# A decay mask moved from TensorE to GpSimd, and the last product's sums taken bank by bank

## The chip, the cores and the metric

The kernel runs on one core of a Trainium2 chip. Its engines are TensorE (PE, matmuls and transposes), VectorE (DVE), ScalarE (ACT), GpSimd (POOL) and SyncE (SP, which issues most of the transfers); each runs its own list of instructions in order, and they meet by semaphores. The metric is the device time of one execution, in microseconds (us).

## The reference

One decoder layer on a sequence of 1024 tokens of width 1024, in fp32. A norm and an input projection feed two groups of heads: differential attention (4 heads) and a gated DeltaNet (4 heads of width 128, in chunks of 64 tokens). Their outputs go through one output projection onto the residual, and a squared-ReLU MLP of hidden width 4096 follows. The parts that the change touches:

```python
g = jnp.cumsum(g, axis=-1)                      # log decay, summed within a chunk
gdiff = g[..., :, None] - g[..., None, :]
decay = jnp.where(tri, jnp.exp(jnp.where(tri, gdiff, 0.0)), 0.0)
Lmat = jnp.where(strict, jnp.einsum('bhncd,bhnjd->bhncj', k_beta, k) * decay, 0.0)
sol = lax.linalg.triangular_solve(Lmat, rhs, left_side=True, lower=True, unit_diagonal=True)
qk = jnp.where(tri, jnp.einsum('bhncd,bhnjd->bhncj', q, k) * decay, 0.0)
```

The MLP is the norm of x, a product with `w_up`, relu squared, a product with `w_down`, and the sum with x. The `decay` matrix is 1 on the diagonal, falls below it, and is 0 above it.

## The kernel before, in words

Every large product is made of three matmuls: each fp32 operand is split into a high and a low part (`hH`, `hL` for activations, `wH`, `wL` for weights), and high x high, low x high and high x low are summed in the same PSUM bank. The kernel works in chunks of 128 rows (P = 128), four to a tile of 512 columns. The stages, by the clock of the trace: 0 to 70 us the norm and the gates; 70 to about 235 the projections of the DeltaNet heads and what prepares their scan; then scan, attention and output projection interleaved until about 620; MLP up until 930; MLP down until the end.

**The decay factors.** A loop over the four heads and two halves (L746 to L760) makes eight tiles `dtm` of 128x512, one 128x128 block for each chunk. ScalarE scales the triangle `tri` by the log decays of the chunk, four instructions for the high parts (`rrh`) and four for the low ones (`rrl`, L752). Two matmuls with the constant triangle `gt_r` (L754, L755) turn them into sums of log decays between two rows, in a bank `ps_e`. Four more matmuls (L757), one for each 128 columns, add `caus`, which is -1e30 above the diagonal, by multiplying it with an identity, both in bf16. ScalarE takes the exponential (L759), so masked places become 0.

**Who reads them.** `dn_proj` (L671) makes the projections of kind 1 (k), 0 (q) and 2 (v) in this order. For each head and half it issues 24 matmuls into a bank `ps_dn` (L267 to L269), of which there are two; ScalarE copies the bank to `cp` (L683), ScalarE and VectorE make the convolution `cy` over four taps (L685, L687), and an activation follows. For k, VectorE makes `k2` (L780), TensorE transposes it (L735) and makes the gram product `ps_m` (L742), and VectorE multiplies the gram by `bp` and by `dtm` (L799), which gives `lt`. GpSimd makes `vsc` beside it (L806). `lt` is stored in blocks to DRAM (`fsx_d`); once all eight are there, `invert` loads them as `fx` (L766), runs 31 steps of two VectorE instructions (L770, L772) and stores the result. `horner` loads it as `gb` (L823), and its first matmuls are L829. For q, VectorE multiplies the gram by `bp` and `dtm` in the same way (L866), which gives `qk`. So `dtm` has two readers, both on VectorE.

**What sets the order.** The instructions of each engine in this stretch are put in order by the scheduler of the Tile framework (`TileContext(schedule_with_timeline_sim=True)`, L1963), which models the times of the program. Only the stretches in a `manual_schedule` (the first 70 us, part of the MLP) keep the order in which they are written; that of the MLP down holds TensorE's order alone. A change of one instruction can therefore move others.

**The end.** `down` (L1847) is one product of the MLP down; 14 of them, each of two halves `s`, use two sets of four banks in turn. `bankB` consists of two tiles of two banks, X1 and X0: t = 0, 1 lie in X1 and t = 2, 3 in X0. A half has 16 pairs (j, t), each of three matmuls (L1863 to L1865), t the bank and j a step of the contraction. In the last half of the last product (`final and s`) t is the outer loop, in all others j is. After the product, four VectorE additions (L1870) take the banks into `acc`, and in the last products a store follows each (L1872). Waits are kept for tiles, so an addition that reads one bank waits for what was issued before it on both banks of its tile, and a matmul into one bank waits for an addition that was issued before it and reads the other bank.

Of the kernel before, what the change touches and what calls it, by code (L numbers as in the profile page):

```python
# [10 lines left out]
F32R = mybir.dt.float32r  # L11
BF16 = mybir.dt.bfloat16
AF = mybir.ActivationFunctionType
ALU = mybir.AluOpType
# [4 lines left out]
P = 128  # L19
# [103 lines left out]
def tile_hymba_layer(  # L123
# [6 lines left out]
    nc = tc.nc  # L130
    V, S, G, T = nc.vector, nc.scalar, nc.gpsimd, nc.tensor

    x2 = x[0]
    out2 = out[0]
# [185 lines left out]
    gp = gpctx.enter_context(tc.tile_pool(name="gp", bufs=1))  # L320
# [147 lines left out]
    tri = sp.tile([P, P], F32, name="tri")  # L468
    gt_f = gp.tile([P, P], F32, name="gt_f")
# [90 lines left out]
    behind = ExitStack()  # L560
    for ins in mark + [x_last]:
        behind.enter_context(tc.issue_after(ins.ins))
    identb = const.tile([P, P], BF16, name="identb")
    V.tensor_copy(identb, ident)
    gt_r = gp.tile([P, P], F32R, name="gt_r")
    V.tensor_copy(gt_r, gt_f)
    caus = const.tile([P, P], BF16, name="caus")
    V.tensor_copy(caus, caus_f)

# [31 lines left out]
    v4 = lambda t: t.rearrange("p (c d) -> p c d", d=P)  # L601
# [59 lines left out]
    def ta(name, bufs, dt=F32):  # L661
        return sa.tile([P, 512], dt, tag=name, name=name, bufs=bufs)
# [66 lines left out]
    def bc_mask(t):  # L729
        return t.unsqueeze(1).broadcast_to([P, 4, P])  # L730
# [15 lines left out]
    for h in range(HEADS):  # L746
        for hf in range(2):
            rh, rl = ta("rrh", 1, F32R), ta("rrl", 1, F32R)
            for t, col in ((rh, ggh), (rl, ggl)):
                for c in range(4):  # L750
                    i = cidx(h, 4 * hf + c)
                    S.activation(t[:, c * P:(c + 1) * P], tri, AF.Copy, scale=col[:, i:i + 1])  # L752
            pse = ph.tile([P, 512], F32, tag="ph", name="ps_e")
            T.matmul(pse, gt_r, rh, start=True, stop=False)  # L754
            T.matmul(pse, gt_r, rl, start=False, stop=False)  # L755
            for c in range(4):
                T.matmul(pse[:, c * P:(c + 1) * P], caus, identb, start=False, stop=c == 3)  # L757
            dtm = sa.tile([P, 512], F32, name=f"dtm{h}{hf}")
            S.activation(dtm, pse, AF.Exp)  # L759
            dts[h, hf] = dtm  # L760

    def invert():
# [15 lines left out]
    for h, hf, y, th in skew(dn_proj(1)):  # L778
# [6 lines left out]
        for c in range(4):  # L785
            i = cidx(h, 4 * hf + c)
# [9 lines left out]
        for c in range(4):  # L796
            i = cidx(h, 4 * hf + c)
# [53 lines left out]
    for h, hf, q2 in skew(dn_proj(0)):  # L851
# [6 lines left out]
        for c in range(4):  # L858
            i = cidx(h, 4 * hf + c)
# [3 lines left out]
        for c in range(4):  # L863
            i = cidx(h, 4 * hf + c)
# [175 lines left out]
    late, accs, over = [], {}, set()  # L1040
# [769 lines left out]
    NK = FF // 2048  # L1810
# [21 lines left out]
    def u_raw(m):  # L1832
        if m < len(halves):
            kg, i, s = halves[m]
            g0 = 4 * kg + 2 * s
            return nc.sync.dma_start(urs[max(m - 1, 0) % 4].rearrange("p (g q) t -> p g q t", g=2),
                                     ud[i][g0:g0 + 2].rearrange("g p q t -> p g q t"))
# [5 lines left out]
    def split4(dst, src):  # L1843
        for j in (0, 2):
            split([x[:, j:j + 2] for x in dst], src[:, j:j + 2])

    def down(kg, wd, i, flip, n, out, start, stop):  # L1847
        bank = bankB if flip ^ (kg % 2) else bankA
        final = kg == NK - 1 and i == 4
        for s in range(2):  # L1850
            v = views[4 * (turn_of[0] % 2):][:4]
            turn_of[0] += 1
            m = halves.index((kg, i, s))
            raw = urs[max(m - 1, 0) % 4]
            split4(v[0:2], raw)
            split4(v[2:4], wd[n][s])
            u_raw(m + 4 if m else 1)
            seq = [(j, t) for t in range(4) for j in range(4)] if final and s else \
                [(j, t) for j in range(4) for t in range(4)]
            for j, t in seq:  # L1860
                sl = slice(t * P, t * P + P)
                s0, s1 = start and s == 0 and j == 0, stop and s == 1 and j == 3
                T.matmul(bank[t], v[0][:, j, sl], v[2][:, j], start=s0, stop=False, skip_group_check=True)  # L1863
                T.matmul(bank[t], v[0][:, j, sl], v[3][:, j], start=False, stop=False, skip_group_check=True)  # L1864
                T.matmul(bank[t], v[1][:, j, sl], v[2][:, j], start=False, stop=s1, skip_group_check=True)  # L1865
        half, ns = out
        for t in range(4):
            tb = t + (4 if half == 0 else 0)
            o = accs[tb][:, ns]
            V.tensor_tensor(o, o, bank[t], ALU.add)  # L1870
            if kg == NK - 1 and i in (2, 3, 7, 4):
                nc.sync.dma_start(out2[tb * P:(tb + 1) * P, ns], o)  # L1872

    u_raw(0)
    for n in "ab":
# [18 lines left out]
    for kg in range(NK):  # L1894
        wd = wds[kg]

        def both(dst, l, r):
            for s in range(2):
                V.tensor_tensor(wd[dst][s], wd[l][s], wd[r][s], ALU.subtract)

        down(kg, wd, 1, 0, "a", (0, lo), True, False)
        both("b", "b", "a")
        down(kg, wd, 5, 1, "b", (1, hi), True, False)
        both("b", "d", "b")
        down(kg, wd, 6, 0, "b", (0, hi), False, False)
        down(kg, wd, 3, 1, "d", (0, hi), False, True)
        both("a", "b", "a")
        down(kg, wd, 7, 0, "a", (1, hi), False, False)
        down(kg, wd, 2, 1, "c", (0, lo), True, True)
        if kg + 1 < NK:  # L1910
            for s in range(2):
                dn_raw(kg + 1, "a", s)
        both("b", "c", "b")
        down(kg, wd, 4, 0, "b", (1, lo), False, True)
        if kg + 1 < NK:
            for n in "bdc":
                for s in range(2):
                    dn_raw(kg + 1, n, s)
# [49 lines left out]
```

## Time and profile before

| | us |
|---|---|
| median of three runs (lowest, highest) | 1227.69 (1225.83, 1229.32) |
| the profiled execution | 1227.74 |
| span of its profile | 1226.0 |
| TensorE busy | 1208.2 |
| VectorE busy | 836.9 |
| ScalarE busy | 624.0 |
| GpSimd busy | 151.9 |

The span is what the profile covers; 1.74 us of the execution lie around it. Columns of the profile rows: start and duration, engine, line of the code, operation, output and inputs with their shapes; in brackets the idle time of that engine just before and what ended it. Matmuls are pipelined, so that the durations of neighbours overlap: what a matmul costs is read from the starts of the rows. A line L1089 or the like is one of the kernel before, if nothing else is said; in the changed kernel the same code stands a line earlier or some lines later.

### The profile page before, as it was taken

Reading aid. Unit: us, or ns where it says so; the run is one execution under the profiler, and the core shown is the slowest. Engines: PE = TensorE matmul, PEld = TensorE weight load, DVE = VectorE, ACT = ScalarE, POOL = GpSimd, SP = SyncE. Lnnn points to the kernel's source line nnn. Section 1 sums busy time; section 2 is a strip of 40 time slices with the busy share of each in tenths; the row PEclk is TensorE's granted clock in tenths of the full one; section 3 lists DMA queues with packets and bytes.
Section 4 is the critical chain, followed back from the end, with each engine's and each line's share of the span. In section 5 each row is a group of like instructions: output and inputs, shape, how many; then the busy total and the mean of one; then the engine's idle time right before and its main releaser. Section 6 shows DMA issues by size and latency. Waiting matters only on the chain.

```text
span 1226.0 us, 18798 instructions
## 1 busy us (share of the span) xinstructions
PE 1208.2 (99%) x6743; PEld 1045.9 (85%) x6743; DVE 836.9 (68%) x1566; ACT 624.0 (51%) x1257; POOL 151.9 (12%) x215
## 2 busy tenths in 40 slices
PE   9999999999998999999999999999999999999998
PEld 7978888899998998888888888888888888888886
DVE  6868797667567667677798554566569755777543
ACT  6588554344355665566766444454563333333330
POOL 2411110035334431002200000000000000000000
PEclk9999999999999999999999999999999999999999
DMA  9334654378748865333628433444479555422301
GB/s 349 105 113 119 169 163 81 84 233 234 249 145 265 244 157 144 79 83 93 204 88 292 155 125 141 165 177 150 154 258 403 214 180 186 150 103 103 137 35 69
DMA packets 179269, 202.12 MB, mean 165 GB/s; under 512 B 63032, under 2 KB 135272, under 8 KB 179176
## 3 DMA queue, kind: packets, MB, share of 16 engines
q1 hardware_dynamic: 174552, 187.28, 48.0%
q0 software_dynamic: 4480, 13.64, 3.0%
q8 instruction: 53, 0.87, 0.3%
q14 instruction: 40, 0.33, 0.1%
q10 hardware_dynamic: 144, 0.00, 0.0%
HBM read 135.86 MB, written 65.01 MB: 164 GB/s over the span
## 4 chain that ended last, share of the span: by engine, by line
PE 91%; ACT 3%; DVE 2%; DMA 2%; SPq 1%; issue 1%; POOL 0%; DVEq 0%; ACTq 0%
PE X L1567 5%; PE X L1565 5%; PE X L1566 5%; PE X L1864 4%; PE X L1863 4%; PE X L1865 4%; PE ps_dn L267 3%; PE ps_qk L1089 3%; PE ps_dn L269 3%; PE ps_dn L268 3%; PE ps_qk L1090 3%; PE ps_qk L1091 3%; PE Y L1567 3%; PE Y L1565 3%; PE Y L1566 3%; PE ps_o L1273 3%
## 5 line engine op out<-in xcount | busy, mean ns | idle before, releaser
L1483 ACT CAST hH<-ur 128x1024 fp32r<-128x1024 f32 x56 | 58.9, 1051 | 173.3 <-PE Y L1864 90.3
L1484 DVE TENSOR_TENSOR hL<-ur,hH 128x1024 fp32r<-128x1024 f32 x56 | 68.4, 1223 | 79.8 <-ACT hH L1483 79.6
L1089 PE MATMUL ps_qk<-wH,hH 128*128 128x256 f32 x384 | 114.5, 298 | 0.7 <-DVE sn L1110 0.7
L1484 DVE TENSOR_TENSOR op<-raw,op 128x1024 fp32r<-128x1024 f32 x48 | 58.7, 1224 | 74.7 <-PE X L1566 40.7
L1090 PE MATMUL ps_qk<-wL,hH 128*128 128x256 f32 x384 | 108.7, 283 | 0.0
L1091 PE MATMUL ps_qk<-wH,hL 128*128 128x256 f32 x384 | 108.6, 283 | 0.0
L1863 PE MATMUL X<-hH 128*128 128x512 f32 x224 | 87.1, 389 | 0.0
L1864 PE MATMUL X<-hL,hH 128*128 128x512 f32 x224 | 87.1, 389 | 0.0
L1865 PE MATMUL X<-hH,hL 128*128 128x512 f32 x224 | 87.1, 389 | 0.0
L267 PE MATMUL ps_dn<-hH,wH 128*128 128x512 f32 x192 | 76.0, 396 | 0.2 <-ACT cp L683 0.2
L268 PE MATMUL ps_dn<-hL,wH 128*128 128x512 f32 x192 | 75.8, 395 | 0.0
L269 PE MATMUL ps_dn<-hH,wL 128*128 128x512 f32 x192 | 75.5, 394 | 0.0
L1089 PEld LDWEIGHTS ps_qk<-wH,hH 128*128 128x128 f32 x384 | 73.6, 192 | 1.4 <-DVE sn L1110 1.1
L1090 PEld LDWEIGHTS ps_qk<-wL,hH 128*128 128x128 f32 x384 | 73.7, 192 | 0.2
L1091 PEld LDWEIGHTS ps_qk<-wH,hL 128*128 128x128 f32 x384 | 73.4, 191 | 0.0
L1484 DVE TENSOR_TENSOR hL<-dw,hH 128x1024 fp32r<-128x1024 f32 x56 | 68.1, 1219 | 0.4 <-ACT hH L1483 0.4
L1483 ACT CAST op<-raw 128x1024 fp32r<-128x1024 f32 x48 | 50.4, 1051 | 35.1 <-PE Y L1567 19.9
L1483 ACT CAST hH<-dw 128x1024 fp32r<-128x1024 f32 x56 | 58.7, 1048 | 10.1 <-DMA dw<-in_w_down_dram 4.4
L1228 ACT ACTIVATE pexp<-pexp,mx 128x128 f32<-128x128 f32 (+7 forms) x64 | 49.6, 775 | 19.6 <-DVE mx L1227 18.7
L687 DVE SCALAR_TENSOR_TENSOR cy<-cp,pv,cy 128x512 f32<-128x512 f32 x72 | 53.7, 747 | 8.1 <-ACT cy L685 7.2
L1389 PE MATMUL ps_op<-wH,hH 128*128 128x512 f32 x128 | 53.3, 416 | 0.0
L1391 PE MATMUL ps_op<-wH,hL 128*128 128x512 f32 x128 | 50.3, 393 | 0.0
(380 smaller groups left out, 3428.7 us busy)
## 6 DMA issues: line engine op xcount, KB each, us to landing
ur<-ud SPq DMA_DIRECT2D x28, 1024.0 KB, 4.9
raw<-in_w_up_dram SPq DMA_DIRECT2D x32, 512.0 KB, 4.0
dw<-in_w_down_dram SPq DMA_DIRECT2D x32, 512.0 KB, 6.6
wraw<-in_w_units_dram SPq DMA_DIRECT2D x48, 256.0 KB, 3.7
qk_d<-qa POOLq DMA_DIRECT2D x32, 256.0 KB, 4.1
ud<-ua SPq DMA_DIRECT2D x16, 512.0 KB, 4.2
ud<-s SPq DMA_DIRECT2D x16, 512.0 KB, 2.6
pka<-park_d SPq DMA_DIRECT2D x32, 192.0 KB, 4.0
```

The costliest lines, as they stand in the source:

```text
L267: T.matmul(ps, lh(k), rh(k), start=(k == 0), stop=False)
L268: T.matmul(ps, lh(k), rl(k), start=False, stop=False)
L269: T.matmul(ps, ll(k), rh(k), start=False, stop=(k == n - 1))
L1089: T.matmul(ps[:, :256], hH[:, k, sl], wh[:, k, :], start=(k == 0), stop=False)
L1090: T.matmul(ps[:, :256], hH[:, k, sl], wl[:, k, :], start=False, stop=False)
L1091: T.matmul(ps[:, :256], hL[:, k, sl], wh[:, k, :], start=False, stop=(k == KB - 1))
L1483: S.copy(dst[0], src)
L1484: V.tensor_tensor(dst[1], src, dst[0].bitcast(F32), ALU.subtract)
L1565: T.matmul(ps, op[0][:, k, cs], h[0][:, k, :], start=start and k == 0, stop=False, skip_group_check=True)
L1863: T.matmul(bank[t], v[0][:, j, sl], v[2][:, j], start=s0, stop=False, skip_group_check=True)
L1864: T.matmul(bank[t], v[0][:, j, sl], v[3][:, j], start=False, stop=False, skip_group_check=True)
L1865: T.matmul(bank[t], v[1][:, j, sl], v[2][:, j], start=False, stop=s1, skip_group_check=True)
```

## The change

The decay loop no longer adds the mask by matmuls. Sums of log decays above the diagonal are empty, so their exponential is 1, and GpSimd multiplies `dtm` in place by `tri`, which is 1 on and below the diagonal and 0 above. The copies of two constants change places. In the last half of the last product the banks are taken in the order 0, 2, 1, 3, and each bank's addition and store are issued right behind its last matmul, by a new inner function `leave`; all other products call `leave` four times after their matmuls, as before.

```diff
--- before.py
+++ after.py
@@ -560,10 +560,10 @@
     behind = ExitStack()
     for ins in mark + [x_last]:
         behind.enter_context(tc.issue_after(ins.ins))
+    gt_r = gp.tile([P, P], F32R, name="gt_r")
+    V.tensor_copy(gt_r, gt_f)
     identb = const.tile([P, P], BF16, name="identb")
     V.tensor_copy(identb, ident)
-    gt_r = gp.tile([P, P], F32R, name="gt_r")
-    V.tensor_copy(gt_r, gt_f)
     caus = const.tile([P, P], BF16, name="caus")
     V.tensor_copy(caus, caus_f)
 
@@ -752,11 +752,10 @@
                     S.activation(t[:, c * P:(c + 1) * P], tri, AF.Copy, scale=col[:, i:i + 1])
             pse = ph.tile([P, 512], F32, tag="ph", name="ps_e")
             T.matmul(pse, gt_r, rh, start=True, stop=False)
-            T.matmul(pse, gt_r, rl, start=False, stop=False)
-            for c in range(4):
-                T.matmul(pse[:, c * P:(c + 1) * P], caus, identb, start=False, stop=c == 3)
+            T.matmul(pse, gt_r, rl, start=False, stop=True)
             dtm = sa.tile([P, 512], F32, name=f"dtm{h}{hf}")
             S.activation(dtm, pse, AF.Exp)
+            G.tensor_tensor(v4(dtm), v4(dtm), bc_mask(tri), ALU.mult)
             dts[h, hf] = dtm
 
     def invert():
@@ -1847,6 +1846,15 @@
     def down(kg, wd, i, flip, n, out, start, stop):
         bank = bankB if flip ^ (kg % 2) else bankA
         final = kg == NK - 1 and i == 4
+        half, ns = out
+
+        def leave(t):
+            tb = t + (4 if half == 0 else 0)
+            o = accs[tb][:, ns]
+            V.tensor_tensor(o, o, bank[t], ALU.add)
+            if kg == NK - 1 and i in (2, 3, 7, 4):
+                nc.sync.dma_start(out2[tb * P:(tb + 1) * P, ns], o)
+
         for s in range(2):
             v = views[4 * (turn_of[0] % 2):][:4]
             turn_of[0] += 1
@@ -1855,7 +1863,7 @@
             split4(v[0:2], raw)
             split4(v[2:4], wd[n][s])
             u_raw(m + 4 if m else 1)
-            seq = [(j, t) for t in range(4) for j in range(4)] if final and s else \
+            seq = [(j, t) for t in (0, 2, 1, 3) for j in range(4)] if final and s else \
                 [(j, t) for j in range(4) for t in range(4)]
             for j, t in seq:
                 sl = slice(t * P, t * P + P)
@@ -1863,13 +1871,11 @@
                 T.matmul(bank[t], v[0][:, j, sl], v[2][:, j], start=s0, stop=False, skip_group_check=True)
                 T.matmul(bank[t], v[0][:, j, sl], v[3][:, j], start=False, stop=False, skip_group_check=True)
                 T.matmul(bank[t], v[1][:, j, sl], v[2][:, j], start=False, stop=s1, skip_group_check=True)
-        half, ns = out
-        for t in range(4):
-            tb = t + (4 if half == 0 else 0)
-            o = accs[tb][:, ns]
-            V.tensor_tensor(o, o, bank[t], ALU.add)
-            if kg == NK - 1 and i in (2, 3, 7, 4):
-                nc.sync.dma_start(out2[tb * P:(tb + 1) * P, ns], o)
+                if final and s1:
+                    leave(t)
+        if not final:
+            for t in range(4):
+                leave(t)
 
     u_raw(0)
     for n in "ab":
```

Three places show how the lists of the engines change. The rows give line, operation, output and inputs, shape, and the engines or queues waited for; numbers behind names count buffers. First GpSimd, from the clearing of `fg` on, where the stretch begins; `vsc` is the square root for which it was used before. Before:

```order
L659 MEMSET fg_940 128x32 [waits Pool_49]
L806 TENSOR_TENSOR vsc_945<-sk_1203,poshalf_108 128x4 [waits DVE_49]
L806 TENSOR_TENSOR vsc_945<-sk_1272,poshalf_108 128x4 [waits DVE_49]
L806 TENSOR_TENSOR vsc_945<-sk_1341,poshalf_108 128x4 [waits DVE_49]
L806 TENSOR_TENSOR vsc_945<-sk_1428,poshalf_108 128x4 [waits DVE_49]
L806 TENSOR_TENSOR vsc_945<-sk_1497,poshalf_108 128x4 [waits DVE_49]
```

After:

```order
L659 MEMSET fg_940 128x32 [waits Pool_49]
L758 TENSOR_TENSOR dtm00_963<-dtm00_963,tri_187 128x512 [waits Activation_49]
L758 TENSOR_TENSOR dtm01_979<-dtm01_979,tri_187 128x512 [waits Activation_49]
L805 TENSOR_TENSOR vsc_945<-sk_1179,poshalf_108 128x4 [waits DVE_49]
L805 TENSOR_TENSOR vsc_945<-sk_1248,poshalf_108 128x4 [waits DVE_49]
L758 TENSOR_TENSOR dtm10_995<-dtm10_995,tri_187 128x512 [waits Activation_49]
L805 TENSOR_TENSOR vsc_945<-sk_1317,poshalf_108 128x4 [waits DVE_49]
L758 TENSOR_TENSOR dtm11_1011<-dtm11_1011,tri_187 128x512 [waits Activation_49]
L758 TENSOR_TENSOR dtm20_1027<-dtm20_1027,tri_187 128x512 [waits Activation_49]
```

The multiplies (L758) stand between the instructions for `vsc`, the first two ahead of all of them; each waits for ScalarE's exponential, and `vsc` queues behind it.

Second VectorE at the beginning of the inverse, the first row of which (L770 before, L769 after) waits for the load of `fx`. Before:

```order
L848 RECIPROCAL small1_72<-vsc_945 128x32 [waits Pool_49]
L687 TENSOR_SCALAR cy_1776<-cp0_946,pv_858,cy_1776 128x512 [waits Activation_49]
L849 TENSOR_TENSOR neg_eg_882<-neg_eg_882,small1_72 128x32 [waits DVE_49]
L687 TENSOR_SCALAR cy_1776<-cp0_946,pv_858,cy_1776 128x512 [waits DVE_49] x2
L866 TENSOR_SCALAR qk_1804<-ps_m_1791,small3_80,dtm00_967 128x128 [waits PE_49]
L866 TENSOR_SCALAR qk_1804<-ps_m_1791,small3_80,dtm00_967 128x128 x3
L292 TENSOR_SCALAR rqt_1801<-small0_71 128x4 [waits Activation_49]
L770 TENSOR_TENSOR ft_941<-fx_939,fg_940 128x31 [waits DMAHW4_49]
```

After:

```order
L865 TENSOR_SCALAR qk_1780<-ps_m_1767,small3_80,dtm00_963 128x128
L848 TENSOR_TENSOR neg_eg_882<-neg_eg_882,small1_72 128x32 [waits DVE_49]
L687 TENSOR_SCALAR cy_1829<-cp1_947,pv_858,cy_1829 128x512 [waits Activation_49]
L687 TENSOR_SCALAR cy_1829<-cp1_947,pv_858,cy_1829 128x512 [waits DVE_49] x2
L865 TENSOR_SCALAR qk_1857<-ps_m_1844,small3_80,dtm01_979 128x128 [waits PE_49]
L865 TENSOR_SCALAR qk_1857<-ps_m_1844,small3_80,dtm01_979 128x128 x3
L292 TENSOR_SCALAR rqt_1854<-small0_71 128x4 [waits Activation_49,Pool_49]
L769 TENSOR_TENSOR ft_941<-fx_939,fg_940 128x31 [waits DMAHW6_49]
```

The rows `qk` of the second half of head 0 (`dtm01`) stood behind the first steps of the inverse and now stand ahead of it; three taps of the convolution stand ahead of it as before.

Third VectorE at the end of the program. `acc` with a tile X1 or X0 is an addition of a bank; a row without brackets waits for nothing. Before:

```order
L1484 TENSOR_TENSOR hL_100<-dw_11016,hH_99 128x2x512 [waits Activation_49]
L1870 TENSOR_TENSOR acc_10123<-acc_10123,X1_8068 128x512 [waits PE_49]
L1870 TENSOR_TENSOR acc_10122<-acc_10122,X1_8068 128x512
L1870 TENSOR_TENSOR acc_10121<-acc_10121,X0_7788 128x512 [waits PE_49]
L1870 TENSOR_TENSOR acc_10120<-acc_10120,X0_7788 128x512
L1963 UNCONDITIONAL_BRANCH
```

After:

```order
L1483 TENSOR_TENSOR hL_100<-dw_10992,hH_99 128x2x512 [waits Activation_49]
L1854 TENSOR_TENSOR acc_10099<-acc_10099,X1_8044 128x512 [waits PE_49]
L1854 TENSOR_TENSOR acc_10097<-acc_10097,X0_7764 128x512 [waits PE_49]
L1854 TENSOR_TENSOR acc_10098<-acc_10098,X1_8044 128x512 [waits PE_49]
L1854 TENSOR_TENSOR acc_10096<-acc_10096,X0_7764 128x512 [waits PE_49]
L1969 UNCONDITIONAL_BRANCH
```

Before, two additions wait, one for the last matmul into each tile; now each waits for TensorE by itself, and they alternate between the tiles.

## The prediction

> **What bounds the kernel now.** I read the page's busy table and chain first, then windows by stage, then the waits of the matrix engine, and only then single rows.
>
> ```profile
> PE 1208.2 (99%) x6743; PEld 1045.9 (85%) x6743; DVE 836.9 (68%) x1566; ACT 624.0 (51%) x1257; POOL 151.9 (12%) x215
> PE 91%; ACT 3%; DVE 2%; DMA 2%; SPq 1%; issue 1%; POOL 0%; DVEq 0%; ACTq 0%
> ```
>
> TensorE is busy 99% of the span and 91% of the chain that ended last: a matmul that is taken out shortens the kernel unless something else then holds TensorE. The two stages that the change touches are the projections of the DeltaNet heads (70 to 190 us) and the end of the MLP. In windows, each column is an engine's busy time in the stretch:
>
> ```profile
> core 0: us, PE busy (x) PEld busy (x) DVE busy (x) ACT busy (x) POOL busy (x), PEclk, DMA share, GB/s
> 70.00:120.00 50.00, 49.45 (x275) 40.53 (x275) 38.19 (x93) 45.52 (x150) 6.98 (x6) 1.00 0.41 110
> 120.00:190.00 70.00, 70.00 (x370) 59.42 (x369) 61.40 (x167) 37.02 (x122) 10.17 (x10) 1.00 0.58 160
> 1100.00:1226.00 126.00, 121.62 (x537) 100.41 (x535) 66.61 (x66) 38.06 (x38) 0.00 (x0) 0.99 0.23 84
> ```
>
> TensorE is full in both early windows at a granted clock of 1.00, so the clock carries no term. VectorE has 50 - 38.19 = 11.8 us free in the first, ScalarE only 4.5. GpSimd is nearly empty. The waits of TensorE in the whole span that lie nearest to the change (total, count, longest):
>
> ```profile
> PE ps_o L1273 <- DVE qa L1055: 2.3, 1, 2.3
> PE ps_qkt L1050 <- DVE om L1291: 1.0, 1, 1.0
> PE ps_p L829 <- ACT W L843: 0.3, 2, 0.2
> PE ps_e L755 <- ACT rrl L752: 0.3, 1, 0.3
> ```
>
> The last two are in the reordered stretch, and small. The first two are in attention, behind it.
>
> **The mask matmuls.** Eight blocks (head, half) lose one group each of four 128x128 bf16 matmuls. Two neighbourhoods of such a group, with start and duration of the first of each row:
>
> ```profile
> 98.91 0.40 PE L755 MATMUL ps_e<-rrl,gt_r 128*128 128x512 f32 x1
> 99.15 0.40 PE L757 MATMUL ps_e<-identb,caus 128*128 128x128 bf16 x4
> 99.35 0.48 PE L267 MATMUL ps_dn<-hH,wH 128*128 128x512 f32 x1
> 99.67 0.39 PE L268 MATMUL ps_dn<-hL,wH 128*128 128x512 f32 x1
> ...
> 85.29 0.48 PE L755 MATMUL ps_e<-rrl,gt_r 128*128 128x512 f32 x1
> 85.61 0.40 PE L757 MATMUL ps_e<-identb,caus 128*128 128x128 bf16 x4
> 85.84 0.39 PE L735 MATMUL ps_t<-ident,k 128*128 128x128 f32 x2
> ```
>
> Durations overlap, so I take differences of starts. In the first place 98.91 to 99.67 is 0.76 us for three steps, L755, the group and L267. A plain step of 512 columns is 0.24 (98.91 to 99.15), so the group costs 0.76 - 2 x 0.24 = 0.28: 0.20 for itself and the rest in a slower L267 behind it. In the second place, with transposes behind, it costs 85.61 to 85.84, 0.23. By what follows them, groups two to eight are five of the first kind and two of the second: 5 x 0.28 + 2 x 0.23 = 1.9 us. The first group is different:
>
> ```profile
> 71.08 0.40 PE L757 MATMUL ps_e<-identb,caus 128*128 128x128 bf16 x4
> 71.73 0.50 PE L267 MATMUL ps_dn<-hH,wH 128*128 128x512 f32 x1 [0.25 <-ACT cp L683]
> 71.11 0.57 ACT L683 COPY cp<-ps_dn 128x512 f32<-128x512 f32 x1
> ```
>
> There L267 waits for a bank that ScalarE empties from 71.11 to 71.68, and ScalarE's order up to that copy stays as it was. So the first group gives 0 (0.23 if the copy also came earlier). Bounds of this term: 0, if something else then holds TensorE (rival 3), and 8 x 0.28 = 2.2; I take **-1.9**, by the rows of the groups themselves.
>
> **The new order of TensorE.** The scheduler also packs the stretch anew. Each passage from transposes and grams (plain fp32) back to the split products costs a little:
>
> ```profile
> 86.88 0.48 PE L267 MATMUL ps_dn<-hH,wH 128*128 128x512 f32 x1
> 87.19 0.39 PE L268 MATMUL ps_dn<-hL,wH 128*128 128x512 f32 x1
> 87.43 0.39 PE L269 MATMUL ps_dn<-hH,wL 128*128 128x512 f32 x1
> ```
>
> The first step takes 0.31 and the next 0.24. So a return costs 0.07. Counted in the two orders, there are 34 returns before and 37 after: 3 x 0.07 = **+0.2**. The gt_r copy is only exchanged with the copy beside it on VectorE, long ahead of its first reader: 0.
>
> **The GpSimd multiplies.** Eight multiplies of 128x512 by 128x512 are added. The nearest row has the same engine, operation, shape and type:
>
> ```profile
> 579.35 1.29 POOL L1420 TENSOR_TENSOR hn<-hn,w2b 128x512 f32<-128x512 f32 x1 [0.88 <-PE ps_o L1273]
> 107.50 0.59 ACT L759 ACTIVATE dtm<-ps_e 128x512 f32<-128x512 f32 x1
> 116.30 1.12 DVE L799 SCALAR_TENSOR_TENSOR lt<-ps_m,small,dtm 128x128 f32<-128x128 f32 x4
> ```
>
> Each costs 1.29 us of an engine that has 43 of 50 us free, 10.3 in all. The multiply stands between exp and the reader lt. The smallest room of the eight is that of head 2, half 1: exp ends at 108.09, lt starts at 116.30, 8.2 us. In the new order the blocks whose room is under 11 us come at most 14 projection matmuls later (head 2, half 0: L755 behind 152 of them and not 138): 14 x 0.24 = 3.4 us, and 8.2 - 3.4 - 1.3 leaves 3.5. What is queued behind a multiply on GpSimd is vsc, which only the inverse's end needs. If this cover were gone, lt would be late, then the stores of its blocks, then the inverse. What it may do to VectorE is a rival below; here **0**, with 10.3 as the upper bound. A gain is excluded, since exp comes no earlier than its own matmuls.
>
> **The inverse.** The last gram moves from behind 236 projection matmuls to behind 251: 15 x 0.24 = 3.6 us later, less the 1.9 saved, is 1.7. Its chain runs over a load, 31 VectorE steps and another load:
>
> ```profile
> 137.34 0.34 SPq L766 DMA_DIRECT2D fx<-fsx_d  x1
> 141.47 0.19 DVE L770 TENSOR_TENSOR ft<-fx,fg 128x31 f32<-128x31 f32 x1 [2.27 <-DMA fx<-fsx_d]
> 197.60 0.71 DVE L825 STREAM_TRANSPOSE W<-gb 128x512 f32<-128x512 f32 x1 [1.94 <-DMA gb<-fsg_d]
> 200.15 1.92 PE L829 MATMUL ps_p<-gb,lt 128*128 128x96 f32 x16
> ```
>
> L829 could start at 197.6 and does at 200.15, 2.55 us of room. One block of qk (1.12, as lt) goes ahead of the first step, and the load of fx (L766) stands behind one more store's issue on SyncE's queue (0.34, as its own): chain up to 1.7 + 1.1 + 0.3 = 3.1 later. L829 itself stands 11 projection matmuls later: 11 x 0.24 - 1.9 = 0.7. So 2.55 + 0.7 = 3.25 is there for 3.1: no new wait, **0**, but with little to spare.
>
> **The tail.** Last product, before:
>
> ```profile
> 1216.22 1.28 DVE L1870 TENSOR_TENSOR acc<-acc,X 128x512 f32<-128x512 f32 x2 [12.77 <-PE X L1865]
> 1221.23 0.39 PE L1865 MATMUL X<-hH,hL 128*128 128x512 f32 x1
> 1221.65 1.28 DVE L1870 TENSOR_TENSOR acc<-acc,X 128x512 f32<-128x512 f32 x2 [4.15 <-PE X L1865]
> ```
>
> A tile holds two banks, so two adds wait for the last matmul (1221.23 + 0.39 = 1221.62), and run one after the other, 0.64 each. Afterwards the third add (bank 1) comes before bank 3's matmuls, and one add of 0.64 stands behind the last. The new waits are of TensorE, for an add on the tile's other bank; each is covered by the 12 matmuls of the bank between, 12 x 0.24 = 2.9 us against 0.64 plus a semaphore. Behind the last add stands one store of the same size as before. Bounds: 0, if the second add's semaphore costs what is saved, and 0.7; I take **-0.6**, the add's own row.
>
> **Sum.** 1227.74 (span 1226.0 and 1.74 around it; the median, 1227.69, is the same to 0.05) - 1.9 + 0.2 + 0 + 0 - 0.6 = **1225.4 us**, -0.2%. Own range 1224.2 (masks 2.2, tail 0.7, both 0.3 waits gone) to 1227.1 (only the tail).
>
> **Rival 1: VectorE is held by the multiplies (slower).** For it, a VectorE addition beside a GpSimd multiply, and another of the same size with GpSimd idle:
>
> ```profile
> 57.94 2.20 POOL L407 TENSOR_TENSOR zg<-zg,dnw 128x252 f32<-128x252 f32 x3 [1.66 <-DVE ab L409]
> 59.45 0.74 DVE L618 TENSOR_TENSOR gu<-ab,dtb 128x32 f32<-128x32 f32 x1
> L628 DVE TENSOR_TENSOR gd<-gd,gte 128x32 f32<-128x32 f32 x1 | 0.2, 193 | 0.0
> ...
> 103.68 0.69 DVE L780 SCALAR_TENSOR_TENSOR k<-cth,cy 128x512 f32<-128x512 f32 x1 [0.70 <-ACT cth L691]
> 105.69 0.60 PE L735 MATMUL ps_t<-ident,k 128*128 128x128 f32 x4
> ```
>
> 0.74 against 0.193: it ended with the multiply (59.45 + 0.74 = 60.19, the GpSimd group at 60.14). The place is k2 (L780) and the taps ahead of it: the transposes start 105.69 - 104.37 = 1.3 us after k2, and one hold is at most 1.29. So a single hold is just absorbed, and it decides once two fall in one block, or one in a block whose room the new order has eaten. All eight unabsorbed: 1225.4 + 10.3 = 1235.7; half: 1230.6. Against it: 11.8 us of VectorE are free there. The Trainium skill ("SBUF — State Buffer", section "Who interferes with whom") states the rule: a VectorE instruction with two SBUF inputs and a GpSimd instruction that reads SBUF exclude each other, and whoever starts first keeps the shared ports for its whole instruction. The rows of L618 and L628 agree. Chance 0.12.
>
> **Rival 2: waits behind the change clear (faster).** Everything after 200 us starts some 2 us earlier against loads and VectorE; if the waits of 2.3 and 1.0 in attention go, 1225.4 - 3.3 = 1222.1. Against: their order of instructions is the same. Chance 0.18.
>
> **Rival 3: the masks were only cover.** ScalarE is busy 45.5 of 50 us there; if it paces the stretch, TensorE waits for cp or rrl what it saved, and only the tail stays: 1227.1. Against: those waits are 0.3 each now. Chance 0.10.
>
> **Rival 4: the inverse comes late.** If its two loads (2.27 and 1.94 waited) take twice as long in the new places, the chain is 4.2 later, less the 0.15 of room: +4.1, 1229.5. Against: both queues go the same way to the same memory as before. Chance 0.10.
>
> **Numbers.** The likeliest has 0.50. A measurement of this kernel can tell 0.3%, 3.7 us: faster is below 1224.0, slower above 1231.4. Faster: most of rival 2 (0.15) and a low edge of the likeliest (0.06), 0.21. Slower: over half of rival 1 (0.08) and a heavier rival 4 (0.03), 0.11. The rest, 0.68. Range 1222.1 (rival 2) to 1230.6 (half of rival 1).
>
> **What would show it.** No L757, 32 fewer matmuls, eight rows of about 1.3 us on GpSimd; no VectorE wait for GpSimd before lt; no TensorE wait over 0.3 between 70 and 220; VectorE rows beside the multiplies of unchanged length (rival 1: longer by up to 1.29, with waits at L735); L829 not waiting for gb (rival 4); one add of 0.64 after the last matmul. The forecast is wrong if TensorE's wait list gains a row above 1 us anywhere.

## The result and the profile after

The changed kernel takes 1224.68 us (median of 16 runs, 1222.68 to 1226.37) against 1227.63 of the kernel before, measured beside it. The ratio is 0.9976, with a 95% interval of 0.9967 to 0.9984: 2.9 us less, 2.0 to 4.1. One of the 16 runs of the kernel before took 2457.7 us, twice as long as the others, and the ratio leaves it out. The forecast was 1225.4, 2.3 us less. A thousandth of the ratio is 1.2 us in what follows. The profiled execution has a span of 1222.9 us, 3.1 below that of before.

The page of the changed kernel, busy times and chain:

```profile
PE 1206.1 (99%) x6711; PEld 1044.5 (85%) x6711; DVE 844.0 (69%) x1566; ACT 623.8 (51%) x1257; POOL 161.7 (13%) x223
PE 89%; ACT 3%; DVE 2%; DMA 2%; SPq 1%; issue 1%; POOL 0%; POOLq 0%; ACTq 0%; DVEq 0%
```

TensorE has 32 matmuls less and still bounds the kernel. VectorE has the same 1566 instructions as before, and yet 7.1 us more of busy time. The windows of the early stage show where that lies:

```profile
core 0: us, PE busy (x) PEld busy (x) DVE busy (x) ACT busy (x) POOL busy (x), PEclk, DMA share, GB/s
70.00:120.00 50.00, 48.84 (x252) 40.88 (x251) 41.27 (x91) 46.62 (x152) 15.56 (x13) 1.00 0.43 117
120.00:190.00 70.00, 70.00 (x370) 59.50 (x369) 63.55 (x166) 38.15 (x124) 11.72 (x11) 1.00 0.58 159
```

GpSimd's share doubles in the first window and VectorE's busy time grows from 38.2 to 41.3 us. The group that grows most is the convolution's taps, three per projection block. Grouped by line, from 70 to 140 us, mean in ns of one, before:

```profile
L687 DVE SCALAR_TENSOR_TENSOR cy<-cp,pv,cy 128x512 f32<-128x512 f32 x30 | 22.3, 747 | 4.3 <-ACT cy L685 3.8
```

After, and below it the tile view of the multiplies (shortest, median and longest in ns):

```profile
L687 DVE SCALAR_TENSOR_TENSOR cy<-cp,pv,cy 128x512 f32<-128x512 f32 x32 | 28.7, 899 | 3.1 <-ACT cy L685 2.5
```

```profile
L758 POOL TENSOR_TENSOR dtm<-dtm,tri x8: 1291/1339/1563, 77.0 to 121.7; 128x512 f32<-128x512 f32 x8
```

Yet no wait of TensorE in the stretch is for VectorE or GpSimd. Its waits after, the two in the changed stretch first:

```profile
PE ps_e L755 <- ACT rrl L752: 0.7, 1, 0.7
PE ps_dn L267 <- ACT cp L683: 0.5, 1, 0.5
PE ps_o L1272 <- DVE qa L1054: 2.3, 1, 2.3
PE ps_qkt L1049 <- DVE om L1290: 1.0, 1, 1.0
```

The first two stood at 0.3 and 0.2 before, and are now above the 0.3 that the prediction allowed between 70 and 220 us. They don't come from the multiplies: the changed kernel without them (e5 below) has 0.5 and 0.5. Gone are the 0.3 us at L829 and one that the prediction had not listed, in attention, before:

```profile
PE ps_qk L1089 <- DVE sn L1110: 0.7, 1, 0.7
```

At the place of a mask group, TensorE's rows after show L755 followed by the next projection step at 0.23 us, and that step is no longer slow:

```profile
94.40 0.39 PE L755 MATMUL ps_e<-rrl,gt_r 128*128 128x512 f32 x1
94.63 0.40 PE L267 MATMUL ps_dn<-hH,wH 128*128 128x512 f32 x1
94.86 0.40 PE L268 MATMUL ps_dn<-hL,wH 128*128 128x512 f32 x1
```

The first block is the exception that was forecast, before (first row) and after:

```profile
70.74 0.50 PE L755 MATMUL ps_e<-rrl,gt_r 128*128 128x512 f32 x1 [0.30 <-ACT rrl L752]
...
71.64 0.49 PE L755 MATMUL ps_e<-rrl,gt_r 128*128 128x512 f32 x1 [0.66 <-ACT rrl L752]
72.63 0.50 PE L267 MATMUL ps_dn<-hH,wH 128*128 128x512 f32 x1 [0.50 <-ACT cp L683]
```

From L755 to L267 it is 0.99 us with and without the masks (70.74 to 71.73 before; the prediction shows the second row). The wait for ScalarE's copy only grew from 0.25 to 0.50.

The end of the program, VectorE and TensorE:

```profile
1216.47 0.69 DVE L1854 TENSOR_TENSOR acc<-acc,X 128x512 f32<-128x512 f32 x1 [2.03 <-PE X L1873]
1219.19 0.69 DVE L1854 TENSOR_TENSOR acc<-acc,X 128x512 f32<-128x512 f32 x1 [2.03 <-PE X L1873]
```

```profile
1218.76 0.39 PE L1873 MATMUL X<-hH,hL 128*128 128x512 f32 x1
```

One addition is left behind the last matmul. From the start of what VectorE does there to the end of the span it is 1222.9 - 1219.19 = 3.71 us; before it was 1226.0 - 1221.65 = 4.35. That is 0.64 less.

### The profile page after: what moved, and what is told of

The parts are those of the page before. It is cut to its first block, busy times and chain, and to the rows that moved or that the text cites. A ratio compares the mean times of both kernels' runs of the same rounds, so it can differ in the third digit from the quotient of the medians.

```text
span 1222.9 us, 18748 instructions
## 1 busy us (share of the span) xinstructions
PE 1206.1 (99%) x6711; PEld 1044.5 (85%) x6711; DVE 844.0 (69%) x1566; ACT 623.8 (51%) x1257; POOL 161.7 (13%) x223
## 4 chain that ended last, share of the span: by engine, by line
PE 89%; ACT 3%; DVE 2%; DMA 2%; SPq 1%; issue 1%; POOL 0%; POOLq 0%; ACTq 0%; DVEq 0%
PE X L1564 5%; PE X L1565 5%; PE X L1566 5%; PE X L1873 4%; PE X L1872 4%; PE X L1871 4%; PE ps_dn L267 3%; PE ps_dn L269 3%; PE ps_dn L268 3%; PE ps_qk L1088 3%; PE ps_qk L1089 3%; PE ps_qk L1090 3%; PE Y L1564 3%; PE Y L1565 3%; PE Y L1566 3%; PE ps_o L1272 2%
## 5 line engine op out<-in xcount | busy, mean ns | idle before, releaser
L1482 ACT CAST hH<-ur 128x1024 fp32r<-128x1024 f32 x56 | 58.8, 1052 | 173.3 <-PE Y L1872 88.6
L1089 PE MATMUL ps_qk<-wL,hH 128*128 128x256 f32 x384 | 108.7, 283 | 0.0
L267 PE MATMUL ps_dn<-hH,wH 128*128 128x512 f32 x192 | 76.0, 396 | 0.5 <-ACT cp L683 0.5
L1089 PEld LDWEIGHTS ps_qk<-wL,hH 128*128 128x128 f32 x384 | 73.4, 191 | 0.2
L687 DVE SCALAR_TENSOR_TENSOR cy<-cp,pv,cy 128x512 f32<-128x512 f32 x72 | 58.4, 812 | 6.1 <-ACT cy L685 5.3
```

Of the source, the lines that this page charges most:

```text
L267: T.matmul(ps, lh(k), rh(k), start=(k == 0), stop=False)
L1089: T.matmul(ps[:, :256], hH[:, k, sl], wl[:, k, :], start=False, stop=False)
L1482: S.copy(dst[0], src)
```

## The experiments

Theory T, that of the prediction: TensorE is the bound; seven mask groups leave it; the multiplies cost nothing because VectorE has room for what they take from it; the tail gives one addition. Its rivals: the masks were only cover; the multiplies cost VectorE something that TensorE feels; the gain is all in the tail. All ratios are against the kernel before, run on the same chip.

**Each part alone.** The first kernel has the decay loop of the changed kernel, with its exchange of the two constants' copies, and the old end; the second the new end and the old loop.

```diff
 e1: before, with
-            for c in range(4):
-                T.matmul(pse[:, c * P:(c + 1) * P], caus, identb, start=False, stop=c == 3)
+            G.tensor_tensor(v4(dtm), v4(dtm), bc_mask(tri), ALU.mult)   # behind the exp
 e2: before, with the new down()
```

> The mask by GpSimd alone, the end of the program as before. Theory of the forecast (TensorE is the bound, seven mask groups of 0.23 to 0.28 us leave it, three dearer returns, multiplies hidden): 1.7 us below the kernel before, about 1.0 us in 1000 us, ratio 0.9986; VectorE busy about 844 us as in the changed kernel; last matmul about 1.7 us earlier, and still two additions behind it. Rival (the gain of the whole change is in the tail, the masks were only cover for ScalarE): ratio 1.000.

> The new end alone, masks by matmul as before. Theory of the forecast: one addition less behind the last matmul, 0.6 us below the kernel before, ratio 0.9995; the end of the profile lies 0.6 to 0.7 us nearer to the last matmul than before (4.8 us from its start). Rival (the additions between hold TensorE for the other bank of the tile): TensorE waits at the start of banks 1 and 3 by 0.7 us each, ratio 1.0005 or more.

Measured: 0.9983 (0.9975 to 0.9992) for the mask, 2.1 us; 0.9995 (0.9984 to 1.0005) for the tail, 0.6 us. They add up to 0.9978, the whole change to 0.9976. By the interval alone the tail can't be told from nothing; the trace of e2 shows it: the last addition starts at 1222.15 and the span ends at 1225.8, 3.65 us as in the changed kernel.

```profile
1222.15 0.69 DVE L1855 TENSOR_TENSOR acc<-acc,X 128x512 f32<-128x512 f32 x1 [2.03 <-PE X L1874]
```

So the gain is not all in the tail. The lists of instructions of e1 are those of the changed kernel up to the end, and those of e2 those of before, which gives two traces of each order. First and last start of two lines mark the stretch, the first projection matmul (L267) and the first transpose of attention (L1050 before, L1049 after). Before:

```profile
L267 PE MATMUL ps_dn<-hH,wH x192: 387/389/501, 58.3 to 225.5; 128*128 128x512 f32 x192
L1050 PE MATMUL ps_qkt<-ident,qn x32: 270/272/330, 251.4 to 426.6; 128*128 128x128 f32 x32
```

After:

```profile
L267 PE MATMUL ps_dn<-hH,wH x192: 387/389/497, 58.8 to 222.5; 128*128 128x512 f32 x192
L1049 PE MATMUL ps_qkt<-ident,qn x32: 270/272/329, 249.8 to 423.1; 128*128 128x128 f32 x32
```

From 58.3 to 251.4 it is 193.1 us (193.5 in e2); from 58.8 to 249.8 it is 191.0 (190.7 in e1). Two more traces with the changed kernel's lists up to the end, e3 and e11 below, have 190.4 and 191.4. The stretch gives 2.4 us between the means; traces of one order lie up to 1.0 us apart.

Added up from the start of each matmul to the start of the next, TensorE's steps of `ps_e` and `ps_dn` take 2.0 us less in the stretch (the mean of these four traces against those two). The inverse's products `ps_p` and `ps_h` take 20.9 us and not 21.4, and the rest is the same to 0.1.

**The price of a mask group.** The kernel before with each group done twice.

```diff
-            for c in range(4):
-                T.matmul(pse[:, c * P:(c + 1) * P], caus, identb, start=False, stop=c == 3)
+            for r in range(2):
+                for c in range(4):
+                    T.matmul(pse[:, c * P:(c + 1) * P], caus, identb, start=False, stop=r == 1 and c == 3)
```

> The kernel before with every mask group done twice (eight bf16 matmuls per block instead of four), nothing else changed; the scheduler packs the stretch anew. Theory of the forecast (a group costs TensorE 0.20 to 0.28 us, and eight of them stand in the way): the second group has no slower step behind it of its own, so 8 x 0.20 = 1.6 us, up to 2.2, above the kernel before, ratio 1.0013 to 1.0018. Rival (the masks were cover, and the gain of the mask part comes from the new order): ratio 1.000.

Measured: 1.0013 (1.0001 to 1.0025), 1.6 us more, eight times 0.20; by the interval it is 0.1 to 3.1 us. A group done twice, and below it one of the kernel before:

```profile
110.40 0.62 PE L758 MATMUL ps_e<-identb,caus 128*128 128x128 bf16 x8
110.83 0.47 PE L269 MATMUL ps_dn<-hH,wL 128*128 128x512 f32 x1
...
110.25 0.40 PE L757 MATMUL ps_e<-identb,caus 128*128 128x128 bf16 x4
110.45 0.48 PE L267 MATMUL ps_dn<-hH,wH 128*128 128x512 f32 x1
```

From the group's start to the next step it is 0.43 us against 0.20, and the stretch is 194.3 us long (58.1 to 252.4), about 1 more than with single groups. The masks were no mere cover. The order of the stretch differs here too, so the numbers are those of groups and order together. The span of this one trace, 1224.5, is shorter than before all the same: from the first transpose of attention to the last matmul it has 967.4 us and before 969.8. No mask stands there, and why it is shorter is open.

**The multiplies: none, two, three.** Here TensorE's, VectorE's, ScalarE's and SyncE's lists are the changed kernel's, and only GpSimd's work differs. The kernel with none (e5) leaves the mask out.

```diff
 e5
-            G.tensor_tensor(v4(dtm), v4(dtm), bc_mask(tri), ALU.mult)
 e9, e4: the same line two and three times
```

> The changed kernel without the multiplies: the part left out is the mask itself. The other engines' lists stay in the changed kernel's order. Theory of the forecast (multiplies hidden): time as the changed kernel's, within 0.5 us, VectorE busy back at about 837 us. Rival (the holds of VectorE cost part of their 7.1 us): 1 to 7 us below the changed kernel.

> The changed kernel with each multiply done twice, the other engines' lists in the changed kernel's order. With the multiply once TensorE loses nothing, done three times it loses 5.6 us (1.0021 against 0.9976 of the kernel before). Theory A (a gradual loss once VectorE's free time is used up, 11.8 us less 7.1 for the first): about 2.5 us above the changed kernel, ratio 0.9996, VectorE busy about 849. Theory B (a threshold per block, 1.3 us of room ahead of the transposes, which two holds in one block exceed): already most of the loss, 4 to 5 us above it, ratio 1.001.

> The changed kernel with each GpSimd multiply done three times (the mask is 0 or 1, the result stays). The lists of the other engines stay in the changed kernel's order. The traces show VectorE's taps of the convolution longer by 7.1 us in all beside the eight multiplies. Theory A (VectorE's holds are only paid from its free time, and there is enough): time as the changed kernel's, within 0.5 us, VectorE busy about 858. Theory B (VectorE has 11.8 us free in the stretch and 7.1 are used up by now; 14.2 more leave 9.5 uncovered): TensorE waits at the transposes or at the projections, 5 to 9.5 us above the changed kernel.

| multiplies per block | ratio to before (95%) | VectorE busy, us | mean tap, ns |
|---|---|---|---|
| 0 (e5) | 0.9975 (0.9967 to 0.9984) | 838.8 | 750 |
| 1 (the change) | 0.9976 (0.9967 to 0.9984) | 844.0 | 899 |
| 2 (e9) | 0.9984 (0.9975 to 0.9992) | 848.3 | 1016 |
| 3 (e4) | 1.0021 (1.0011 to 1.0030) | 853.9 | 1060 |

One multiply costs nothing that can be seen: without it the time is the same, with about 1 us of uncertainty on either ratio and 190.9 us for the stretch. VectorE's busy time falls by 5.2 us without it (844.0 to 838.8), so of the 7.1 us of growth 1.9 are not the multiplies'. The second costs about 1 us (its interval overlaps that of the first), the third 4.5 more. The loss is not in proportion to VectorE's busy time, which grows by about 5 us each time; it begins late and then rises fast. Neither theory written for two multiplies (2.5 us, or 4 to 5) had it so small. The waits of TensorE with three multiplies, in the changed stretch:

```profile
PE ps_t L735 <- DVE k L781: 2.2, 2, 1.7
PE ps_dn L267 <- ACT cp L683: 1.0, 2, 0.5
PE ps_t L735 <- ACT k L695: 0.9, 1, 0.9
PE ps_e L755 <- ACT rrl L752: 0.7, 1, 0.7
```

With two there is a single wait for k2, of 0.4 us. One such place with three, VectorE, GpSimd and TensorE:

```profile
104.05 1.65 DVE L781 SCALAR_TENSOR_TENSOR k<-cth,cy 128x512 f32<-128x512 f32 x1
```

```profile
103.84 1.31 POOL L759 TENSOR_TENSOR dtm<-dtm,tri 128x512 f32<-128x512 f32 x1
105.22 1.61 POOL L760 TENSOR_TENSOR dtm<-dtm,tri 128x512 f32<-128x512 f32 x1
```

```profile
105.75 0.66 PE L735 MATMUL ps_t<-ident,k 128*128 128x128 f32 x4 [0.45 <-DVE k L781]
```

k2, 0.69 us when alone, takes 1.65: it starts inside a multiply (103.84 to 105.15) and ends 0.55 after it. The next multiply then takes 1.61 and not 1.3, since it starts while k2 still runs. That is the place that rival 1 of the prediction named.

**Held, or only late?** With three multiplies the mask also comes 2.6 us later or more. This kernel delays it by GpSimd instructions that read nothing.

```diff
+            for _ in range(6):
+                G.memset(v4(dtm)[0:32, :, 32:], 0.0)
             G.tensor_tensor(v4(dtm), v4(dtm), bc_mask(tri), ALU.mult)
```

> The changed kernel with six GpSimd clears ahead of each multiply, of places that the mask makes 0 anyway. They write and read nothing, and hold the multiply back by about as long as the two further multiplies did (2.7 us), so the mask is ready as late, but GpSimd reads no more than in the changed kernel. Theory A (the loss with three multiplies came from VectorE held by GpSimd's reads): time as the changed kernel's within 1 us, VectorE busy about 844, taps of about 0.90 us. Theory B (the loss came from the mask being late for the gram products): about 5 us above the changed kernel, VectorE waiting for GpSimd ahead of lt. Theory C (any GpSimd instruction holds VectorE): taps of over 1.0 us and a loss as with three multiplies.

The places cleared lie, in fact, on the side that the mask keeps (in `tri` as it is stored a partition keeps the columns from its own number on), so this kernel changes part of the decay factors; its instructions and waits are those meant. Measured: 0.9976 (0.9967 to 0.9986), the changed kernel's ratio. The clears in its tile view, and the taps by line:

```profile
L759 POOL MEMSET dtm<- x48: 407/409/427, 77.2 to 125.3; 32x384 f32 x48
```

```profile
L687 DVE SCALAR_TENSOR_TENSOR cy<-cp,pv,cy 128x512 f32<-128x512 f32 x31 | 24.8, 807 | 3.8 <-ACT cy L685 3.3
```

48 clears of 0.41 us are 19.6 us of GpSimd, and VectorE's busy time is 843.3, as in the changed kernel. A mask that comes 2.5 us later or more costs nothing, and these GpSimd instructions, which only write, do not hold VectorE. The taps even fall to 0.81, since the multiply now falls beside other instructions (k2 grows from 0.69 to 0.84). Nor was the mask late for its reader: neither here nor with three multiplies does VectorE wait for GpSimd ahead of `lt`, and the mask is ready at least 1.9 us before it. So what cost 5.5 us with three multiplies was VectorE being held by GpSimd's reads. The Trainium skill states the rule behind it ("SBUF — State Buffer", section "Who interferes with whom": GpSimd and the second input of a VectorE instruction share ports, and an instruction of GpSimd that only writes does not contend). The runs agree: taps of 0.75 us took 0.90 beside the multiplies, and the clears added nothing to VectorE's busy time.

**The multiply on VectorE.**

```diff
-            G.tensor_tensor(v4(dtm), v4(dtm), bc_mask(tri), ALU.mult)
+            V.tensor_tensor(v4(dtm), v4(dtm), bc_mask(tri), ALU.mult)
```

> The changed kernel with the eight multiplies on VectorE and not on GpSimd. A VectorE instruction of this size takes 0.68 us in the trace, 5.5 us in all, against 7.1 us by which VectorE's own instructions grow beside GpSimd's multiplies. Theory A (VectorE's free time pays in both cases): time as the changed kernel's within 1 us, VectorE busy about 843. Theory B (a multiply in VectorE's queue waits for the exponential and holds what is behind it): TensorE waits at the transposes, 1 to 5 us above the changed kernel.

Measured: 0.9986 (0.9975 to 0.9997). That is 1.2 us above the changed kernel's ratio, with intervals that overlap, and the order of the stretch is another one. By line, 70 to 140 us, and the waits of TensorE that are new:

```profile
L758 DVE TENSOR_TENSOR dtm<-dtm,tri 128x512 f32<-128x512 f32 x8 | 5.5, 687 | 0.3 <-ACT dtm L757 0.2
```

```profile
PE ps_h L836 <- DVE pb L831: 0.9, 1, 0.9
PE ps_h L836 <- DVE W L840: 0.3, 1, 0.3
```

The waits are behind the inverse, not at the transposes as theory B had it. Whether they come from the multiplies or from the order is open.

**The order of the last banks.**

```diff
-            seq = [(j, t) for t in (0, 2, 1, 3) for j in range(4)] if final and s else \
+            seq = [(j, t) for t in range(4) for j in range(4)] if final and s else \
```

> The changed kernel with the banks of the last half in the order 0, 1, 2, 3, each addition still behind its bank. Theory of the forecast (an addition holds the matmuls of the other bank of its tile, and only the bank between covers it): TensorE waits twice, at banks 1 and 3, by 0.7 us and a semaphore each, 1.5 to 2 us above the changed kernel. Rival (banks of a tile are independent): no wait, as the changed kernel.

Measured: 0.9995 (0.9985 to 1.0004), 2.3 us above the changed kernel's ratio. Of TensorE's waits at the end there is one row:

```profile
PE X L1871 <- DVE acc L1854: 1.6, 2, 0.8
```

Two waits of 0.8 us, at banks 1 and 3. The alternation hides them; without it the new end would be 1.0 us worse than the old one by the traces (1.6 - 0.64), and 1.5 by the ratios of e3 and e1.

**A shorter last store.** The last bank's addition and store are made in two halves of 256 columns.

```diff
+            if final and t == 3:
+                for c, q in ((0, nc.sync), (256, nc.scalar)):
+                    V.tensor_tensor(o[:, c:c + 256], o[:, c:c + 256], bank[t][:, c:c + 256], ALU.add)
+                    q.dma_start(out2[tb * P:(tb + 1) * P, ns][:, c:c + 256], o[:, c:c + 256])
+                return
```

> The changed kernel with the last bank's addition and store in two halves of 256 columns, the second store from ScalarE's queue. If the store's time goes with its size, the end comes 0.2 to 0.4 us earlier than in the changed kernel (3.7 us from the start of the last addition to the end there); if it is all fixed cost, the same to 0.1 us later. Ratio 0.997 to 0.9978, and only the trace can tell.

Measured: 0.9980 (0.9968 to 0.9991), not to be told from the changed kernel. In its trace the end comes 1225.2 - 1221.77 = 3.43 us after the start of the addition, 0.28 less than the changed kernel's 3.71:

```profile
1221.77 0.75 DVE L1856 TENSOR_TENSOR acc<-acc,X 128x256 f32<-128x256 f32 x2 [2.03 <-PE X L1878]
```

## Why the prediction was right

Forecast -2.3 us, measured -2.9 with an interval that holds it. What it named as the source, the mask groups and the last addition, is what gave the time; the stretch gave 0.7 us more than the -1.7 of its terms. By its steps:

- **Masks, -1.9.** Right: the steps of `ps_e` and `ps_dn`, where the groups stood, gave 2.0 of the stretch's 2.4, and e1 by its ratio 2.1. The groups are worth what their rows said: e6 pays 0.20 for each by its ratio (wide as the interval is) and 0.23 in its rows, and where one stood, the slow L267 behind it is gone. The first block gave nothing, for the reason named.
- **Three dearer returns, +0.2.** This is the term that failed. Projection triples that follow a gram number 15 in the timelines of both kernels, and those that follow the inverse's products 5 before and 6 after: one dearer return, 0.08, and not three. How the count in the lists came to three is open.
- **The small waits.** The 0.3 at L829 went, which stood only in the lower end of the range. The inverse's products, with these waits, gave 0.45 of the 2.4. They are as short in e6 (20.9 us), which has every mask twice: this part came with the new order of the stretch and not from the masks, and the prediction's sum had no gain from the order.
- **Multiplies, 0.** Right (e5). But the row on which the duration rested was not the whole price: the eight multiplies take 11.1 us of GpSimd and about 5 of VectorE (844.0 against 838.8 in e5). The sign that VectorE's rows beside them keep their length failed. Rival 1's mechanism was there, though without its waits at L735, and was paid from VectorE's 11.8 free us. The point from which it decides was put at two holds in a block, and two multiplies per block are where the loss begins.
- **Inverse, 0** (and rival 4). Right: L829's successor, L828, starts without a wait, though the room computed was small.
- **Tail, -0.6.** Measured -0.64 in the trace, 0.6 by the ratio of e2.
- **Rival 2** (two later waits clear) fell: 2.3 and 1.0 stand unchanged in all traces. Another wait of attention (L1089), 0.7 before and 0.4 in e2, is gone wherever the order of the stretch is a new one, in e6 too, whose attention starts 1.0 us later than before. So an earlier start, the mechanism of rival 2, is not what removes it; what does is open. The prediction's list of waits did not have it.
- **Rival 3** (masks as cover) holds for the first block alone; e1 (2.1 us less with the old end) and e6 speak against it for the rest.

## What to carry to other kernels

A few small matmuls in the way of a full TensorE are worth the difference of the starts around them, and not their durations. Work that is moved to GpSimd has to be charged to VectorE too, when both read SBUF: here it cost VectorE as much as doing the work itself (5.5 us on VectorE, about 5 in holds), and what decided here is VectorE's room ahead of the next matmul that needs it, block by block. An addition that is issued early for one bank of a tile holds the next matmul into the other bank, unless other banks are taken in between.

## What was not expected of the hardware

The holds go both ways, and reach small instructions with one input. With three multiplies, GpSimd's second and third took 1.62 us in the median and not 1.3, and this VectorE instruction on 128x4 numbers, 0.17 us when alone, waited for a multiply from 113.26 to 114.89:

```profile
113.65 1.26 DVE L790 TENSOR_SCALAR sk<-small 128x4 f32<-128x4 f32 x1
```

```profile
113.26 1.63 POOL L760 TENSOR_TENSOR dtm<-dtm,tri 128x512 f32<-128x512 f32 x1
```
